# Prompt attention: even and odd key tiles of the value sums on the two column halves of TensorE

## The chip, the cores and the metric

The kernel runs on one core of one Trainium2 chip. The metric is the device time of one execution in microseconds (us). Each kernel is timed in several executions, and the median counts. One execution is also taken by the hardware profiler, and all rows of the trace come from that one.

## What is computed

The reference is one inference step of a decoder trunk of two layers, for a prompt of 1024 tokens and for a sample group of 8 sequences with 8 tokens each. The part that the change touches is the stick-breaking attention of the prompt in the first layer (8 heads of 64 channels, queries in blocks of 128, strictly causal). For each head and each block of queries it is, cut to what matters:

```python
z = jnp.einsum('nqhd,nkhd->nhqk', qblk, k) * scale + bias_f
mask = k_pos[None, :] < pblk[:, None]
log_1m = jnp.where(mask, jax.nn.log_sigmoid(-z), 0.0)
after = lax.cumsum(log_1m, axis=3, reverse=True) - log_1m
logw = jnp.where(mask, jax.nn.log_sigmoid(z) + after, -jnp.inf)
wgt = jnp.exp(logw)
return jnp.einsum('nhqk,nkhd->nqhd', wgt.astype(v.dtype), v)
```

The last line is the value sum: the weights of a block of 128 queries against all keys up to it, times the values of those keys. Around it stand the layer's projections, a convolution branch, the sample group's attention over a paged cache, output projections and feed-forward layers, all in float32.

## The kernel before

The program is one long stream of TensorE matmuls for the projections and feed-forward layers, in which weights are split into a high and a low part (tile `hl`, lines 184 to 197, ScalarE and GpSimd) and multiplied in three terms (`mm3`, line 235). Other work, which is called background here, is cut into pieces and put between those matmuls by hand: the generator `attention` (lines 937 to 1048) does a piece and yields, and the main stream asks for the next piece at fixed slots (`bg`, line 341). So each engine has a fixed order of instructions, written by the order in which Python issues them, and an engine that waits holds up all that is queued behind it.

Prompt attention runs in two halves: `attention(GA)` for the query blocks 0 to 3 (in the trace from about 230 to 338 us, beside the input projection of the second token group), `attention(GB)` for the blocks 4 to 7 (from there to about 564 us, beside the output projection and the feed-forward layer of the first token group). A unit is one head `h` and one query block `i`; it has i + 1 key tiles of 128 keys. The units of a half go head after head and within a head from the largest block down, so GA has 8 times (4, 3, 2, 1) key tiles, GB 8 times (8, 7, 6, 5).

Four stages work on a unit, one step of the loop in line 1029 apart:

- `s1(u)`: scores `z` by TensorE (line 982), and two sigmoids of them by ScalarE into `q` and `be` (line 987).
- `s2(u)`: VectorE runs the cumulative product backwards over the keys (`q`, lines 996 and 999, two scans) and multiplies it into `be` (line 1001).
- `s3(u)`: TensorE transposes `be` key tile by key tile (line 1011), ScalarE copies the result into `wt` (line 1012).
- `s4(u)`: TensorE adds up `vrow.T @ wt` over the key tiles into the PSUM tile `o` of 64 x 128 (line 1020), ScalarE copies `o` into the head's rows of `qall`, which is the upper half of `hb` (line 1021).

One step issues `s4(u - 3)`, `s3(u - 2)`, `s2(u - 1)` and `s1(u)`, with 12 matmuls of the main stream in between; for GB these 12 are cut in two groups of 6, one before `s1`, one behind. `o` has one buffer (`op_`, bufs=1), so the next unit's value sum may begin only when `o` has been read. `wt` also has one buffer, `q2` and `be` have two. The PE's instruction stream shows each float32 matmul of line 1020 as two records, so a unit of 8 key tiles has 16.

VectorE also serves the main stream: it moves accumulators `acc` out of PSUM (lines 291 and 295), forms low parts (lines 241 and 382), and prepares the next head's operands (lines 962 and 965). GpSimd forms the weights' low parts (line 186). The sample group's attention later in the program has, in `pv` (line 1210), matmuls to the row halves 0 to 63 and 64 to 127 of one PSUM tile, one after the other; they are not changed, but the prediction reads them.

Of the kernel before, what the change touches and what calls it, by code (L numbers as in the profile page):

```python
# [8 lines left out]
F = mybir.dt.float32  # L9
FR = mybir.dt.float32r  # L10
I32 = mybir.dt.int32
AF = mybir.ActivationFunctionType
OP = mybir.AluOpType
# [44 lines left out]
def trunk_kernel(ctx, tc, x_prompt, x_sample, cache_k, cache_v, state_conformer, state_shortconv, state_pool,  # L58
# [4 lines left out]
    pe, act, dve, pool, sp = nc.tensor, nc.scalar, nc.vector, nc.gpsimd, nc.sync  # L63
# [158 lines left out]
    def w_next(live=0):  # L222
        j = wj[0]
        wj[0] += 1
        w_split(j + 3 - live)
        w_load(need(j + 6 - live))
        return hls.pop(j)
# [408 lines left out]
    def accs():  # L636
        return accbox["p"].tile([128, len(accbox["g"].blocks), 512], F, name="acc")
# [8 lines left out]
    qall = hb[:, 4:8]  # L646
# [290 lines left out]
    def attention(g):  # L937
# [3 lines left out]
        with ExitStack() as es_:  # L941
            pa = es_.enter_context(tc.tile_pool(name=f"pa{g.c0}", bufs=1))
            zp = es_.enter_context(tc.tile_pool(name=f"zp{g.c0}", bufs=1, space=PSUM, side="right"))
            op_ = es_.enter_context(tc.tile_pool(name=f"op{g.c0}", bufs=1, space=PSUM, side="right"))
# [4 lines left out]
            kt_, qa, vrow, small = {}, {}, {}, []  # L949
# [64 lines left out]
            def s4(u):  # L1014
                h, i = units[u]
                hp, hh = divmod(h, 2)
                w = wt.pop(u)
                o = op_.tile([64, 128], F, name="o2")
                for j in range(i + 1):
                    pe.matmul(o, vrow[h][:, j], w[:, j], start=j == 0, stop=j == i)  # L1020
                act.activation(qall[hh * 64:hh * 64 + 64, hp, i * 128:i * 128 + 128], o, AF.Copy)

            load_v(0)
            operands(0)
# [4 lines left out]
            for u in range(len(units) + 3):  # L1029
                if u >= 3:  # L1030
                    s4(u - 3)
                if 2 <= u < len(units) + 2:
                    s3(u - 2)
                if 1 <= u < len(units) + 1:
                    s2(u - 1)
                if g is GB:
                    yield 1
                if u < len(units):
                    h, r = divmod(u, 4)
                    if r == 0 and h < 7:  # L1040
                        operands(h + 1)
                    if r == 2 and h < 7:
                        load_v(h + 1)
                    s1(u)
                for _ in range(2):
                    if small:
                        small.pop(0)()
                yield 1
# [672 lines left out]
    for n in range(2, KC):  # L1721
        h = w_next()
        a = accs()
# [4 lines left out]
    with tc.tile_pool(name="fab", bufs=1) as ep:  # L1728
        gen = forms_a(ep)
        for n in range(KC):  # L1730
            h = w_next()
            a = accs()
# [256 lines left out]
```

## Time and profile before

| what | value |
|---|---|
| median of 3 runs | 2576.84 us |
| lowest and highest run | 2574.14 and 2580.19 us |
| the profiled execution's own time | 2575.97 us |
| its span, first to last instruction | 2574.2 us |
| busy: TensorE matmul (PE), weight load (PEld) | 96% and 86% of the span |
| busy: VectorE (DVE), ScalarE (ACT), GpSimd (POOL) | 66%, 43%, 61% |
| mean granted TensorE clock | 0.994 |
| value sums, line 1020 | 576 matmul records, 238 to 564 us |

Shares of busy time are means over stages with different limits. Matmuls are pipelined, so the durations of neighbouring matmul records overlap, and the time that a run of them takes is read from the start of the first to the start of what comes next. In the rows of the timeline the first number is the start in us from the span's start, the second the time from the first start to the last end of the merged instructions; a bracket gives the idle time of the engine before it and who ended it. Rows of a window give its length, then the busy time of PE, PEld, DVE, ACT and POOL with the number of instructions, then granted clock, DMA share and GB/s.

### The profile page before, as it was taken

The page shows a single profiled execution, that of the slowest core. Times are in us where ns is not written, and L with a number is a line of the kernel's source. Part 1 is how long each engine was busy: PE and PEld are TensorE (multiplying, and loading weights), DVE is VectorE, ACT ScalarE, POOL GpSimd, SP SyncE. Part 2 cuts the span into 40 slices and gives each one's busy share as a digit, 9 for nine tenths or more (in the row PEclk, how much of TensorE's full clock was granted, in tenths as well). Part 3 has the DMA queues.
Part 4 walks back from the last instruction along what each step waited for, and adds up shares of the span by engine and source line. Part 5 has one row for each costly group of instructions (what it writes and reads, how often), then busy time and mean ns, then how long its engine had stood idle before and what let it go on. Part 6 is the DMA issues. An engine that isn't in the chain of part 4 may idle for free.

```text
span 2574.2 us, 41142 instructions
## 1 busy us (share of the span) xinstructions
PE 2477.7 (96%) x15727; PEld 2213.7 (86%) x15727; DVE 1693.0 (66%) x2359; ACT 1105.3 (43%) x1875; POOL 1564.2 (61%) x1205
## 2 busy tenths in 40 slices
PE   8999999999999999999999999999999998999998
PEld 6788877887777668989999889989888887999997
DVE  3696777968867734467666633348776778666655
ACT  5536766754444334334333522234434434443333
POOL 6754243544434346678777722266888885887775
PEclk9999999999999999999999999999999999999999
DMA  7342231224555434222323411152233332333322
GB/s 220 113 113 74 64 109 46 70 83 142 157 162 160 139 107 152 74 74 83 99 83 98 130 42 46 38 161 65 84 91 96 95 96 82 107 95 103 99 83 78
DMA packets 355484, 258.30 MB, mean 100 GB/s; under 512 B 22913, under 2 KB 303617, under 8 KB 355272
## 3 DMA queue, kind: packets, MB, share of 16 engines
q1 hardware_dynamic: 355256, 255.66, 33.8%
q8 instruction: 125, 2.05, 0.3%
q14 instruction: 71, 0.58, 0.1%
q10 hardware_dynamic: 32, 0.01, 0.0%
HBM read 237.41 MB, written 18.69 MB: 99 GB/s over the span
## 4 chain that ended last, share of the span: by engine, by line
PE 44%; DVE 8%; POOL 2%; issue 1%; ACT 1%; POOLq 0%; DVEq 0%; ACTq 0%
PE acc L235 23%; PE acc L521 20%; POOL hl L197 1%; DVE sum L200 1%; DVE hid L241 1%; DVE hb L295 1%; DVE sum L201 1%; DVE b L1669 0%; DVE tmp L525 0%; DVE sum L202 0%; DVE x L1669 0%; DVE sum_c L214 0%; DVE fb L1673 0%; DVE xs L1673 0%; POOL tmp L500 0%
## 5 line engine op out<-in xcount | busy, mean ns | idle before, releaser
L186 POOL TENSOR_TENSOR hl<-stage,hl 128x512 fp32r<-128x512 f32 x464 | 634.7, 1391 | 475.1 <-ACT hl L184 357.0
L235 PE MATMUL acc<-x,hl 128*128 128x512 f32 (+1 forms) x3648 | 780.6, 350 | 12.2 <-DVE hb L295 2.6
L235 PEld LDWEIGHTS acc<-x,hl 128*128 128x128 f32 x3648 | 581.4, 189 | 77.2 <-issue 10.9
L235 PE MATMUL acc<-hid,hl 128*128 128x288 f32 (+1 forms) x3096 | 552.3, 334 | 16.8 <-DVE hb L295 6.9
L235 PEld LDWEIGHTS acc<-hid,hl 128*128 128x128 f32 x3096 | 470.4, 190 | 69.9 <-DVE hb L295 11.0
L295 DVE TENSOR_TENSOR hb<-acc,hb 128x512 f32<-128x512 f32 (+1 forms) x360 | 256.4, 718 | 184.8 <-PE acc L235 183.4
L521 PE MATMUL acc<-x,hl 128*128 128x288 f32 (+1 forms) x2676 | 362.4, 290 | 6.0 <-ACT x L1792 2.0
L521 PEld LDWEIGHTS acc<-x,hl 128*128 128x128 f32 x2676 | 349.0, 188 | 8.4 <-POOL hl L197 2.7
L197 POOL TENSOR_TENSOR hl<-sum,hl 128x512 fp32r<-128x512 f32 x180 | 237.1, 1344 | 168.6 <-ACT hl L196 168.5
L184 ACT ACTIVATE hl<-stage 128x1024 fp32r<-128x1024 f32 x232 | 243.5, 1055 | 218.5 <-PE acc L235 129.6
L525 DVE TENSOR_TENSOR tmp<-acc,tmp 128x288 f32<-128x288 f32 (+1 forms) x420 | 173.5, 441 | 228.0 <-ACT tmp L537 135.3
L197 POOL TENSOR_TENSOR hl<-stage,hl 128x512 fp32r<-128x512 f32 x180 | 267.0, 1505 | 13.3 <-ACT hl L196 13.3
L521 PE MATMUL acc<-b,hl 128*128 128x256 f32 (+1 forms) x1548 | 216.6, 291 | 14.1 <-DVE tmp L525 11.2
L521 PEld LDWEIGHTS acc<-b,hl 128*128 128x128 f32 x1548 | 202.3, 189 | 19.6 <-ACT hl L196 12.7
L235 PE MATMUL acc<-x1t,hl 128*128 128x288 f32 x1152 | 216.4, 296 | 1.5 <-POOL hl L186 1.5
L235 PEld LDWEIGHTS acc<-x1t,hl 128*128 128x128 f32 x1152 | 196.0, 188 | 19.4 <-POOL hl L186 1.7
L196 ACT ACTIVATE hl<-sum 128x512 fp32r<-128x512 f32 x180 | 103.1, 623 | 237.9 <-DVE sum L202 217.6
L291 DVE TENSOR_TENSOR tmp<-acc,rr 128x512 f32<-128x512 f32 (+1 forms) x108 | 75.0, 709 | 113.2 <-PE acc L235 100.0
L500 POOL TENSOR_TENSOR tmp<-tmp 128x576 f32<-128x576 f32 (+1 forms) x85 | 127.8, 1504 | 11.7 <-ACT tmp L477 8.3
L196 ACT ACTIVATE hl<-stage 128x512 fp32r<-128x512 f32 x180 | 105.6, 618 | 67.5 <-PE acc L235 62.3
L241 DVE TENSOR_TENSOR hid<-tmp,hid 128x512 fp32r<-128x512 f32 (+1 forms) x88 | 99.1, 1127 | 44.0 <-ACT hid L240 41.2
L235 PE MATMUL acc<-x1a,hl 128*128 128x512 f32 x480 | 121.7, 407 | 2.5 <-POOL hl L186 1.3
(289 smaller groups left out, 3242.9 us busy)
## 6 DMA issues: line engine op xcount, KB each, us to landing
stage<-in_w_ffn_in_dram SPq DMA_DIRECT2D x176, 512.0 KB
stage<-in_w_ffn_out_dram SPq DMA_DIRECT2D x88, 512.0 KB
stage<-in_w_in_even_dram SPq DMA_DIRECT2D x40, 512.0 KB
kst<-in_cache_k_dram SPq DMA_DIRECT2D x64, 256.0 KB
vst<-in_cache_v_dram SPq DMA_DIRECT2D x64, 256.0 KB
stage<-in_w_out_even_dram SPq DMA_DIRECT2D x16, 512.0 KB
stage<-in_w_in_odd_dram SPq DMA_DIRECT2D x16, 512.0 KB
stage<-in_w_out_odd_dram SPq DMA_DIRECT2D x16, 512.0 KB
```

The lines of the kernel that those rows point to most:

```text
L184: act.activation(hl[:, 0], st, AF.Copy)
L186: pool.tensor_tensor(hl[:, 1, c], st[:, c], f32(hl[:, 0, c]), op=OP.subtract)
L196: act.activation(hl[:, 0, c], x, AF.Copy)
L197: pool.tensor_tensor(hl[:, 1, c], x, f32(hl[:, 0, c]), op=OP.subtract)
L200: todo = [lambda: dve.tensor_tensor(sb, su[:, lo], su[:, hi], op=OP.add), lambda: dve.tensor_tensor(sa[:, hi], sg[:, lo], su[:, lo], op=OP ...
L235: pe.matmul(acc[:, b, :c1 - c0], w, xs[:, xi, c0 - o:c1 - o], start=first and s == 0, stop=last and s == 2)
L241: (on or dve).tensor_tensor(dst[:, 1], src, f32(dst[:, 0]), op=OP.subtract)
L291: dve.tensor_tensor(d, a, r, op=OP.mult)
L295: dve.tensor_tensor(d, a, d, op=OP.add)
L500: (dve if both and f == NF - 1 else pool).tensor_tensor(t[:, :n], t[:, :n], u[:, :n], op=OP.mult)
L521: pe.matmul(acc[:, :w2], h[:, wi, i, k], xk[:, xi], start=k == 0 and s == 0, stop=k == 3 and s == 2)
L525: dve.tensor_tensor(out, acc[:, :w2], x, op=OP.add)
```

## The change

Only `s4` is changed. The PSUM tile is 128 x 128 instead of 64 x 128. Key tile j goes to its lower 64 partitions where j is even and to its upper 64 where j is odd, which puts the matmul on the one or the other column half of the array; each half accumulates its own sum (so the first matmul of each half starts it, and the last of each half stops it). Where a unit has one key tile, ScalarE copies as before. Elsewhere ScalarE copies the odd half into a new SBUF tile `ot` (two buffers), and VectorE adds the even half from PSUM to it and writes the result to `qall`.

```diff
-                o = op_.tile([64, 128], F, name="o2")
+                o = op_.tile([128, 128], F, name="o2")
                 for j in range(i + 1):
-                    pe.matmul(o, vrow[h][:, j], w[:, j], start=j == 0, stop=j == i)
-                act.activation(qall[hh * 64:hh * 64 + 64, hp, i * 128:i * 128 + 128], o, AF.Copy)
+                    pe.matmul(o[j % 2 * 64:j % 2 * 64 + 64], vrow[h][:, j], w[:, j], start=j < 2, stop=j >= i - 1)
+                r = slice(hh * 64, hh * 64 + 64)
+                a = qall[r, hp, i * 128:i * 128 + 128]
+                if i == 0:
+                    act.activation(a, o[0:64], AF.Copy)
+                    return
+                t = pa.tile([128, 128], F, name="ot", bufs=2)
+                act.activation(t[r], o[64:128], AF.Copy)
+                dve.tensor_tensor(a, o[0:64], t[r], op=OP.add)
```

On TensorE, ScalarE, GpSimd and SyncE the instructions stand in the same order as before, with the same counts; ScalarE's copy of line 1021 is now that of line 1027 (or 1024 for one key tile). VectorE has 56 instructions more, one for each unit but the 8 with one key tile.

On VectorE in the first half of attention (GA), in a step with a unit of four key tiles, the difference is this (`qz` is the next head's operand, the number in `o_2256` is that of the buffer; the order names a scan SCALAR_TENSOR_TENSOR where the trace says TENSOR_TENSOR_SCAN):

```order
 L1001 TENSOR_TENSOR be<-be,q_2196 128x383
 L965 TENSOR_TENSOR qz_2107<-hb,qa 64x512
+L1028 TENSOR_TENSOR hb<-o_2256,ot 64x128
 L996 SCALAR_TENSOR_TENSOR q_2231<-q_2231,ident 128x128
 L999 SCALAR_TENSOR_TENSOR q_2231<-q_2231,ones 128x128
 L1001 TENSOR_TENSOR be<-be,q_2231 128x255
```

The sum of the older unit, three steps behind, stands ahead of the scans of the unit that is one step behind.

On VectorE in the second half (GB), the order before over three steps of a head reads as follows.

```order
L965 TENSOR_TENSOR qz_3521<-hb,qa 64x512
L996 SCALAR_TENSOR_TENSOR q_4822<-q_4822,ident 128x128
L999 SCALAR_TENSOR_TENSOR q_4822<-q_4822,ones 128x640
L1001 TENSOR_TENSOR be<-be,q_4822 128x767
L291 TENSOR_TENSOR tmp<-acc,rr 128x512
L996 SCALAR_TENSOR_TENSOR q_4871<-q_4871,ident 128x128
L999 SCALAR_TENSOR_TENSOR q_4871<-q_4871,ones 128x512
L1001 TENSOR_TENSOR be<-be,q_4871 128x639
L996 SCALAR_TENSOR_TENSOR q_4931<-q_4931,ident 128x128
```

And the same place with the change:

```order
L965 TENSOR_TENSOR qz_3569<-hb,qa 64x512
L1028 TENSOR_TENSOR hb<-o_4923,ot 64x128
L996 SCALAR_TENSOR_TENSOR q_4910<-q_4910,ident 128x128
L999 SCALAR_TENSOR_TENSOR q_4910<-q_4910,ones 128x640
L1001 TENSOR_TENSOR be<-be,q_4910 128x767
L291 TENSOR_TENSOR tmp<-acc,rr 128x512
L1028 TENSOR_TENSOR hb<-o_4978,ot 64x128
L996 SCALAR_TENSOR_TENSOR q_4961<-q_4961,ident 128x128
L999 SCALAR_TENSOR_TENSOR q_4961<-q_4961,ones 128x512
L1001 TENSOR_TENSOR be<-be,q_4961 128x639
L1028 TENSOR_TENSOR hb<-o_5036,ot 64x128
L996 SCALAR_TENSOR_TENSOR q_5023<-q_5023,ident 128x128
```

Each step's first scan now has the add ahead of it.

ScalarE's order in those steps, with the change, shows what stands ahead of the copy that the add needs:

```order
L1027 ACTIVATE ot<-o_4978 64x128
L1012 ACTIVATE wt<-m 128x512
L1012 ACTIVATE wt<-m 128x256
L184 ACTIVATE hl<-stage 128x1024
L987 ACTIVATE q_5023<-z_5018,bh 128x1024
L987 ACTIVATE be<-z_5018,bh 128x1024
L959 ACTIVATE kt<-kall 64x1024
L960 ACTIVATE qa<-hb 64x512
L1027 ACTIVATE ot<-o_5036 64x128
```

Nothing moved here; before, the copies of line 1021 stood in these places.

## The prediction

> **What bounds the kernel now.** I read the profile's page first.
>
> ```profile
> span 2574.2 us, 41142 instructions
> PE 2477.7 (96%) x15727; PEld 2213.7 (86%) x15727; DVE 1693.0 (66%) x2359; ACT 1105.3 (43%) x1875; POOL 1564.2 (61%) x1205
> ```
>
> TensorE is busy nearly all the time, but this is a mean. What the value sums are worth is read from the stretch in which they stand. So next came the value sums' own line: its matmuls, and who waited for them.
>
> ```profile
> L1020 PE MATMUL o<-wt,vrow x576: 272/273/325, 238.2 to 563.7; 128*64 128x128 f32 x192
> ACT hb L1021: 35.2, 34
> ```
>
> ScalarE's copy is the only one that often waits for them (35.2 us in 34 waits); it is on no critical path so far, because nothing near needs its result. Then the table by stretch, one row for each head of the second half, from the first value sum of a head to that of the next (length, then busy PE, PEld, DVE, ACT, POOL):
>
> ```profile
> 359.00:384.54 25.54, 23.97 (x144) 19.72 (x143) 24.50 (x20) 17.45 (x29) 15.49 (x12) 1.00 0.31 83
> 384.54:409.87 25.33, 25.33 (x149) 20.85 (x149) 20.26 (x19) 17.72 (x29) 13.30 (x12) 1.00 0.20 53
> 409.87:449.75 39.88, 36.59 (x196) 28.54 (x195) 28.88 (x33) 25.03 (x40) 12.69 (x13) 1.00 0.14 40
> 449.75:474.39 24.64, 24.20 (x143) 19.71 (x142) 23.62 (x19) 18.74 (x30) 15.92 (x14) 1.00 0.31 86
> 474.39:498.33 23.94, 23.94 (x144) 19.74 (x143) 20.88 (x19) 16.88 (x28) 9.59 (x12) 1.00 0.20 55
> 498.33:522.26 23.93, 23.93 (x144) 19.73 (x143) 20.78 (x19) 17.11 (x28) 9.56 (x11) 1.00 0.20 56
> 522.26:546.19 23.93, 23.93 (x143) 19.73 (x142) 19.94 (x23) 14.50 (x24) 8.24 (x10) 1.00 0.15 45
> 546.19:563.80 17.61, 17.61 (x111) 14.54 (x110) 8.93 (x9) 7.41 (x15) 5.91 (x6) 1.00 0.21 60
> ```
>
> TensorE fills five of these heads without a gap, so its time is the heads' length there. But VectorE is close behind: 20.8 of 23.9 us in the two middle ones, 24.50 of 25.54 and 23.62 of 24.64 in two others, where TensorE already has gaps. The clock is 1.00 and the DMA share at most 0.31, so neither limits. Nothing later runs to a fixed time; what TensorE gains here stays.
>
> **What is removed: TensorE time.** The timeline gives the runs of line 1020, first for one head of the first half, then for one of the second:
>
> ```profile
> 302.19 1.09 PE L1020 MATMUL o<-wt,vrow 128*64 128x128 f32 x8
> 305.51 0.87 PE L1020 MATMUL o<-wt,vrow 128*64 128x128 f32 x6
> 308.75 0.65 PE L1020 MATMUL o<-wt,vrow 128*64 128x128 f32 x4
> 312.08 0.43 PE L1020 MATMUL o<-wt,vrow 128*64 128x128 f32 x2
> ...
> 498.33 1.96 PE L1020 MATMUL o<-wt,vrow 128*64 128x128 f32 x16
> 504.54 1.74 PE L1020 MATMUL o<-wt,vrow 128*64 128x128 f32 x14
> 510.75 1.52 PE L1020 MATMUL o<-wt,vrow 128*64 128x128 f32 x12
> 516.50 1.31 PE L1020 MATMUL o<-wt,vrow 128*64 128x128 f32 x10
> ```
>
> Each record costs 0.109 us ((1.96 - 1.09) / 8). Do two column halves run at the same time? The same program has a case: the sample group's matmuls alternate between the two halves.
>
> ```profile
> 679.37 1.94 PE L1210 MATMUL o<-vst,wts 128*64 128x512 f32 x8
> ```
>
> Eight records of 512 columns, at 4 x 0.109 = 0.436 us each, would take 7 x 0.436 + 0.59 = 3.64 us one behind another (0.59 being one record alone); as four pairs 3 x 0.436 + 0.59 = 1.90. The row says 1.94: they run in pairs. So a run's time becomes that of its longer half. For 8, 7, 6, 5 key tiles these are 4, 4, 3, 3 tiles, that is 8, 8, 6, 6 records: 1.96, 1.74, 1.52, 1.31 become 1.09, 1.09, 0.87, 0.87, which saves 0.87, 0.65, 0.65, 0.44, in all 2.61 us a head. For 4, 3, 2, 1 key tiles it saves 0.44, 0.22, 0.22 and 0, in all 0.88. Eight heads each: 20.9 + 7.0 = 27.9 us. The surplus of 0.04 us over four slots would, on 320 slots, take back 3.2 at most; I take none, since a like start is in the rows of line 1020 already.
>
> **What is added: 56 adds on VectorE.** No row has this form (64 x 128, one input from PSUM). The nearest:
>
> ```profile
> L1149 DVE TENSOR_TENSOR zs<-z,zs x24: 410/540/552, 589.5 to 891.5; 64x384 f32<-64x384 f32 x16, 64x264 f32<-64x264 f32 x8
> L965 DVE TENSOR_TENSOR qz<-hb,qa x16: 677/689/1769, 229.8 to 523.8; 64x512 fp32r<-64x512 f32 x16
> L291 DVE TENSOR_TENSOR tmp<-acc,rr x10: 677/686/693, 444.7 to 562.8; 128x512 f32<-128x512 f32 x10
> L996 DVE TENSOR_TENSOR_SCAN q<-q,ident x64: 406/420/1539, 232.1 to 554.3; 128x128 f32<-128x128 f32 x64
> ```
>
> Line 1149 is the same operation on 264 and 384 columns: 0.410 and about 0.540 us, a slope of 0.0011 us a column, so 0.26 to 0.27 for 128. The far bound is line 996, also 128 columns wide, which takes up to 1.54 us when it meets GpSimd. I take 0.27, since line 291, with one input from PSUM like the add, never left 0.677 to 0.693, while line 965, with both inputs in SBUF, went to 1.77. That is 56 x 0.27 = 15.1 us of VectorE, 1.08 in a head of the second half. With 1.54 it would be 86 us.
>
> [...]
>
> ScalarE's copy keeps its size and place: no cost. GpSimd, SyncE and the DMA queues keep their order. TensorE's next value sum now also waits for the add, since `o` has one buffer; that is a whole step later (5 to 6 us), so it costs nothing.
>
> **The new wait.** Before, VectorE's scans of the unit one step behind started whenever VectorE was free. Now the add stands ahead of them, and it waits for ScalarE's copy, which waits for this step's value sum and for all that ScalarE has queued. Behind it wait the scans, the product `be`, and the accumulators' moves; TensorE's transposes of the next step wait for `be`. I worked through the head from 498.33, from VectorE's, ScalarE's and GpSimd's timelines and TensorE's transposes:
>
> ```profile
> 505.25 1.13 DVE L996 TENSOR_TENSOR_SCAN q<-q,ident 128x128 f32<-128x128 f32 x1
> 508.64 0.82 DVE L1001 TENSOR_TENSOR be<-be,q 128x639 f32<-128x639 f32 x1
> 510.60 1.54 DVE L996 TENSOR_TENSOR_SCAN q<-q,ident 128x128 f32<-128x128 f32 x1 [1.14 <-ACT q L987]
> 514.39 1.23 DVE L1001 TENSOR_TENSOR be<-be,q 128x1023 f32<-128x1023 f32 x1
> 517.67 0.69 DVE L241 TENSOR_TENSOR hid<-tmp,hid 128x512 fp32r<-128x512 f32 x1 [0.73 <-ACT hid L240]
> 521.19 2.00 DVE L1001 TENSOR_TENSOR be<-be,q 128x895 f32<-128x895 f32 x1
> ```
> ```profile
> 505.37 0.63 ACT L474 ACTIVATE tmp<-tmp 128x512 f32<-128x512 f32 x1 [0.65 <-DVE tmp L291]
> 506.31 0.27 ACT L1021 ACTIVATE hb<-o 64x128 f32<-64x128 f32 x1 [0.32 <-PE o L1020]
> 513.08 0.25 ACT L1021 ACTIVATE hb<-o 64x128 f32<-64x128 f32 x1
> ```
> ```profile
> 508.86 3.00 POOL L186 TENSOR_TENSOR hl<-stage,hl 128x512 fp32r<-128x512 f32 x2 [1.41 <-ACT hl L184]
> ```
> ```profile
> 512.20 0.77 PE L1011 MATMUL m<-ident,be 128*128 128x128 f32 x5
> 517.74 1.09 PE L1011 MATMUL m<-ident,be 128*128 128x128 f32 x8
> ...
> 524.15 0.98 PE L1011 MATMUL m<-ident,be 128*128 128x128 f32 x7
> ```
>
> Step from 504.54: the copy cannot start before line 474 has ended (506.0), so copy and add end at 506.58; the scan before started at 505.25, so it is 1.33 late. Its `be` ended at 509.46, the transposes came at 512.20: 2.74 of slack, of which TensorE's own gains in this step and the next take 1.30. What is left, 1.44, covers it.
>
> Step from 510.75: ScalarE is busy until the copy at 513.08 to 513.33, and this is not TensorE's doing. The add ends at 513.60; the scan started at 510.60, before TensorE had even begun this value sum. It is 3.0 late. It then no longer meets GpSimd's line 186 (over at 511.86), which may give back 1.13 (1.54 against 0.41): 1.87. Slack: 517.74 - 515.62 = 2.12, less 1.09 of gains: 1.03. TensorE stalls 0.84.
>
> Step from 516.50: 1.03 of lateness is left, a gap of 0.73 on VectorE takes most of it, the add brings 0.27: 0.57. Slack: 524.15 - 523.19 = 0.96, less gains of 1.31: -0.35. TensorE stalls 0.92. The fourth step has slack enough.
>
> So of 2.61 us the head keeps 2.61 - 0.84 - 0.92 = 0.85. In VectorE's terms its length becomes 23.08 = 20.78 + 1.08 + 1.22, where 1.22 is the waiting that the add brings.
>
> **The sum.** I carry that to the other heads: new length is the larger of (length - 2.61) and (VectorE's busy time + 1.08 + 1.22). In the order of the rows above the gains are -1.26, 2.61, 2.61, -1.28, 0.76, 0.85, 1.69, 2.61: 8.6 us. In the first half the gain lies between 0 and 0.88 a head. Its low end is seen here, where the transposes already follow `be` by 0.06 us and every gain turns into waiting:
>
> ```profile
> 242.55 0.42 DVE L1001 TENSOR_TENSOR be<-be,q 128x255 f32<-128x255 f32 x1
> ...
> 243.03 0.44 PE L1011 MATMUL m<-ident,be 128*128 128x128 f32 x2 [0.58 <-DVE be L1001]
> ```
>
> I take 0.3, nearer to this row, since the add delays VectorE in these steps too: 2.4 us. Together 11.0 us. The profiled execution (2575.97, its span 2574.2 and 1.8 around it) would come to 2565.0; the median, 0.87 higher, to 2565.8.
>
> **Rivals.** A measurement of this kernel can tell about 0.2%, 5.2 us, from no change.
>
> (1) *TensorE keeps nearly all.* The waits for the copy vanish into gaps, as VectorE's lateness also delays what GpSimd and ScalarE do. With 0 in place of 1.22 the heads give 0, 2.61, 2.61, -0.06, 1.98, 2.07, 2.61, 2.61, in all 14.4, and the first half 7.0: 21.4 us, 2555.4. For it: the one 1.13 shows that GpSimd's meetings can move either way. Against it: the copy at 513.08 is late through ScalarE alone.
>
> (2) *Slower: VectorE, waiting for ScalarE's copy, becomes the bound.* If no lateness is absorbed, a head of VectorE grows by 0.27 + 1.33 + 3.0 + 0.27 = 4.87, so waiting is 3.8 in place of 1.22. The heads give -3.84, 0.19, 2.61, -3.86, -1.82, -1.73, -0.89, 2.61: -6.7, the first half 0, so 2583.5. It decides from a waiting of about 2.7 us a head. For it: the two heads with VectorE at 24.50 and 23.62 us have no room at all; against it: 1.14 and 0.73 us gaps in the head above. [...]
>
> (3) *The halves do not run together here*, because a 128-column pass hides two weight loads less well than line 1210's 512. Then the 27.9 us are gone; the lateness costs 2.5 us in the two full heads and about 0.5 in five others: 2581.8. Against it: line 1210.
>
> (4) *Nearly nothing*: waits between my 1.22 and rival 2's, within 5 us of before.
>
> **Numbers.** Forecast (5 to 17 us less) 0.48; (1) 0.15; (2) 0.16; (3) 0.04; (4) 0.17. Faster 0.63, same 0.18 (with a part of (3)), slower 0.19. The range leaves out little of (1) and the far part of (2): 2554 to 2582.
>
> **What would show it.** Line 1020's runs of 16 records at about 1.1 us prove the pairing; 1.9 would prove rival 3. The add of 64 x 128 should show 0.27 us and wait for line 1027 in most steps; TensorE's transposes should wait for `be` in several steps of each head, by 1 to 2 us. If these waits are absent, rival 1 holds; if VectorE is busy or waiting for ScalarE without a gap through most heads, rival 2.

## The result and the profile after

The changed kernel takes 2590.4 us (median of 4 runs, 2588.63 to 2592.99) against 2576.49 before (4 runs). The ratio is 1.0052, with a 95% interval of 1.0037 to 1.0068: slower by half a per cent, where 11 us less had been forecast. The profiled execution has a span of 2587.4 us, 13.2 more than before. Three executions of the kernels tried below, whose granted clock fell to between 0.65 and 0.85, are left out of every median and ratio.

The page after, first lines:

```profile
span 2587.4 us, 41236 instructions
PE 2460.0 (95%) x15727; PEld 2195.4 (85%) x15727; DVE 1701.4 (66%) x2415; ACT 1107.9 (43%) x1875; POOL 1565.6 (61%) x1205
```

TensorE's busy time fell by 17.7 us while the span grew by 13.2: TensorE has less to do and waits more. (Line 1020 alone fell by more, from 76.6 to 48.9 us.) VectorE's busy time rose by 8.4 us only, less than the adds themselves take, so its other operations became 7.5 us shorter together. Half of that is line 500, long after attention (6.9 to 3.2 us); of attention's own lines the product (1001) lost 3.5 us and the long scan (999) gained 2.3.

The value sums' line, their runs of 16 and 14 records in the timeline, and the add's line:

```profile
L1020 PE MATMUL o<-wt,vrow x576: 272/273/325, 237.6 to 579.8; 128*64 128x128 f32 x192
...
536.29 1.09 PE L1020 MATMUL o<-wt,vrow 128*64 128x128 f32 x16
546.86 1.09 PE L1020 MATMUL o<-wt,vrow 128*64 128x128 f32 x14
```
```profile
L1028 DVE TENSOR_TENSOR hb<-o,ot x56: 271/283/286, 238.9 to 580.4; 64x128 f32<-64x128 f32 x56
its engine sat idle before it (us, times) until:
  ACT ot L1027: 42.0, 28
```

The pairing is there in full: 1.96 and 1.74 us became 1.09 and 1.09. The add costs 0.283 us. But VectorE stood still for 42.0 us in front of it, waiting for ScalarE's copy. And the waits behind it show who pays: TensorE's transposes wait 37.1 us for the product `be` (us in all, times, longest), against 3.0 us in 3 waits before. Here the row before, then the row after:

```profile
PE m L1011 <- DVE be L1001: 3.0, 3, 1.6
```
```profile
PE m L1011 <- DVE be L1001: 37.1, 33, 3.7
```

The first value sum starts 0.6 us earlier than before, the last 16.1 us later (579.8 against 563.7).

By heads of the second half, from one head's first value sum to the next one's, as before:

```profile
364.79:390.04 25.25, 21.57 (x144) 17.12 (x143) 21.14 (x21) 16.68 (x27) 14.31 (x13) 1.00 0.32 85
390.04:418.36 28.32, 24.49 (x149) 19.55 (x149) 21.65 (x23) 18.52 (x30) 10.19 (x11) 0.94 0.21 58
418.36:459.25 40.89, 35.36 (x195) 27.05 (x194) 29.62 (x39) 25.72 (x40) 11.58 (x12) 0.96 0.11 32
459.25:488.14 28.89, 23.90 (x144) 19.30 (x143) 24.88 (x23) 19.80 (x31) 15.49 (x13) 0.88 0.26 73
488.14:511.51 23.37, 21.45 (x143) 17.14 (x142) 20.07 (x23) 17.13 (x28) 11.41 (x12) 1.00 0.21 57
511.51:536.29 24.78, 21.39 (x143) 17.12 (x143) 20.45 (x23) 17.23 (x28) 10.36 (x11) 1.00 0.19 54
536.29:562.85 26.56, 22.90 (x143) 18.44 (x143) 23.83 (x27) 14.60 (x24) 8.56 (x10) 0.94 0.12 41
```

These seven heads took 25.54, 25.33, 39.88, 24.64, 23.94, 23.93 and 23.93 us before. Two are shorter now (by 0.29 and 0.57), five longer (by 2.99, 1.01, 4.25, 0.85, 2.63). In each longer one, TensorE and VectorE both have gaps (24.49 and 21.65 busy of 28.32): neither is the bound, they wait for each other in turn. And in four of them the granted clock is below 1.00, which it was in none before.

How the turn looks in the first half, in TensorE's, ScalarE's, VectorE's and again TensorE's timeline of the changed kernel:

```profile
300.49 0.44 PE L1020 MATMUL o<-wt,vrow 128*64 128x128 f32 x4
```
```profile
300.68 0.62 ACT L960 ACTIVATE qa<-hb 64x512 fp32r<-64x512 f32 x1
301.32 0.28 ACT L1027 ACTIVATE ot<-o 64x128 f32<-64x128 f32 x1
```
```profile
301.63 0.28 DVE L1028 TENSOR_TENSOR hb<-o,ot 64x128 f32<-64x128 f32 x1 [2.71 <-ACT ot L1027]
...
308.32 1.09 DVE L996 TENSOR_TENSOR_SCAN q<-q,ident 128x128 f32<-128x128 f32 x1
309.44 1.31 DVE L999 TENSOR_TENSOR_SCAN q<-q,ones 128x128 f32<-128x128 f32 x1
310.86 0.42 DVE L1001 TENSOR_TENSOR be<-be,q 128x255 f32<-128x255 f32 x1
```
```profile
311.34 0.44 PE L1011 MATMUL m<-ident,be 128*128 128x128 f32 x2 [0.94 <-DVE be L1001]
```

VectorE idles 2.71 us. For the first 2.0 of them the value sum is not done (it ends at 300.93): TensorE is itself late, having stood still for 1.35 us at 298.06 for an earlier `be`. Only the next 0.4 us are ScalarE's, which does the next head's operands (line 960) ahead of the copy, and the last 0.3 are the copy. From here VectorE works without a gap: two steps on, the scans run beside GpSimd (1.09 and 1.31 us; with GpSimd idle the same forms took 0.41 at 298.12 and 0.48 at 296.99) and TensorE waits 0.94 us for `be`. And the worst place, in the second half:

```profile
534.33 0.28 DVE L1028 TENSOR_TENSOR hb<-o,ot 64x128 f32<-64x128 f32 x1
534.65 1.56 DVE L996 TENSOR_TENSOR_SCAN q<-q,ident 128x128 f32<-128x128 f32 x1
536.25 2.65 DVE L999 TENSOR_TENSOR_SCAN q<-q,ones 128x768 f32<-128x768 f32 x1
538.93 1.97 DVE L1001 TENSOR_TENSOR be<-be,q 128x895 f32<-128x895 f32 x1
```
```profile
534.64 2.64 POOL L186 TENSOR_TENSOR hl<-stage,hl 128x512 fp32r<-128x512 f32 x2 [4.03 <-DVE hb L1028]
...
537.28 2.68 POOL L500 TENSOR_TENSOR tmp<-tmp 128x512 f32<-128x512 f32 x1
```
```profile
541.05 1.73 PE L1011 MATMUL m<-ident,be 128*128 128x128 f32 x7 [3.66 <-DVE be L1001]
```

Here the add does not wait itself; VectorE is still late from the add before, which waited 2.10 us for its copy (at 527.46). The late scan meets GpSimd for its whole length, and TensorE stands still for 3.66 us. Then the transposes themselves are slow: 1.73 us for 7 where before the row read 0.98. The window that follows shows why (length, then the five busy times, then the granted clock):

```profile
541.00:544.40 3.40, 3.35 (x12) 3.00 (x13) 3.30 (x6) 1.07 (x2) 0.00 (x0) 0.51 0.02 5
544.40:549.00 4.60, 4.60 (x35) 3.74 (x34) 3.58 (x7) 2.12 (x4) 0.10 (x1) 1.00 0.00 0
```

The clock is 0.50 for 3.4 us, from 540.9, just ahead of the stall's end, to 544.3. In these heads the same came with the stalls of 2.79, 2.60 and 3.51 us that end at 393.97, 445.64 and 463.85: 0.50 from 394.2 to 397.5, from 445.4 to 448.7 and, for 6.8 us, from 462.4 to 469.2. Around those of 2.43 and 2.29 us that end at 368.31 and 514.90 it stayed at 1.00. What sets the slow clock off is not shown here.

### The profile page after: what moved, and what is told of

Its sections match the earlier page's. It is cut to its first block, busy times and chain, and to the rows that moved or that the text cites. A ratio compares the mean times of both kernels' runs of the same rounds, so it can differ in the third digit from the quotient of the medians.

```text
span 2587.4 us, 41236 instructions
## 1 busy us (share of the span) xinstructions
PE 2460.0 (95%) x15727; PEld 2195.4 (85%) x15727; DVE 1701.4 (66%) x2415; ACT 1107.9 (43%) x1875; POOL 1565.6 (61%) x1205
## 4 chain that ended last, share of the span: by engine, by line
PE 43%; DVE 9%; POOL 2%; issue 1%; ACT 1%; POOLq 0%; DVEq 0%; ACTq 0%
PE acc L235 23%; PE acc L521 19%; POOL hl L197 1%; DVE sum L200 1%; DVE hid L241 1%; DVE hb L295 1%; DVE sum L201 1%; DVE sum L202 0%; DVE tmp L525 0%; DVE sum_c L214 0%; DVE b L1676 0%; POOL tmp L500 0%; DVE fb L1680 0%; PE blk L1899 0%; DVE x L1676 0%
```

## The experiments

Three theories stood. A: the add stands ahead of the scans and makes them wait for ScalarE's copy. B: VectorE has no room for 56 more operations, wherever they stand. C: the value sums' PSUM tile has one buffer, and the next value sum waits for the add. In a kernel's edit, `sums_` is a list of held-back adds: the add of line 1028 becomes

```diff
-                dve.tensor_tensor(a, o[0:64], t[r], op=OP.add)
+                sums_.append(lambda: dve.tensor_tensor(a, o[0:64], t[r], op=OP.add))
```

and `while sums_: sums_.pop(0)()` issues it at the place named.

**The add at the end of the step's attention work** (the two lines behind `s2(u - 1)` in the loop).

> The add of the changed kernel is issued at the end of the step's VectorE work for attention, behind the scans and the product be, in place of ahead of them; everything else is as in the changed kernel. Theory A (the add, standing ahead of the scans, makes them wait for ScalarE's copy, and the transposes wait for be): VectorE's wait for line 1027 falls from 42 us to under 8, TensorE's wait for be from 38 us to under 15, and most of the 27.9 us of TensorE time is kept: 2552 to 2563 us. Theory B (VectorE is simply too full for 56 more operations, 15.9 us, wherever they stand): 2585 to 2592, as with the change. Theory C (the PSUM tile of the value sums has one buffer, and the next value sum waits for the add): above 2590, with a wait of TensorE for the add in the trace.

2571.67 us against 2574.82; ratio 0.9986 (0.9976 to 0.9996). All three theories missed the time. The waits of TensorE between 229 and 590 us:

```profile
PE o L1021 <- DVE hb L1029: 11.3, 9, 2.2
PE o L1021 <- ACT qa L964: 6.4, 4, 1.7
PE m L1012 <- DVE be L1002: 2.6, 2, 2.4
...
PE o L1021 <- ACT be L988: 1.2, 2, 0.9
PE o L1021 <- ACT hl L184: 1.2, 1, 1.2
```

A is right on `be` (2.6 us in place of 37.1), and C is right on what replaces it: the value sums (line 1021 here) wait for the add that frees their PSUM tile. The profile puts 11.3 us down to the add and 8.8 to ScalarE, but all 16 value sums of these rows start 0.10 to 0.15 us behind the end of an add, so this wait is 20.1 us. B is out: the same 56 adds stand here in a kernel that is 0.66%, some 17 us, faster than the changed one.

**The add between the scans and `be`** (the two lines in `s2`, ahead of line 1001).

> The add is issued between the scans and the product be. Theory A: by then the copy has been done nearly everywhere, so be is late only by the add's own 0.28 us: 2553 to 2565 us, 0 to 4 us above the kernel with the add behind be. Theory B: 2585 to 2592. Theory C: between the changed kernel and the kernel with the add behind be, since the PSUM tile is freed between the two.

2557.61 us; ratio 0.9934 (0.9920 to 0.9948). In A's range of time; but A had put it 0 to 4 us above the kernel with the add behind `be`, and C between that kernel and the changed one, and it is 0.52% below the former. Where the change waited for 42.0 us, this kernel's add waits 9.4, and TensorE waits 7.8 us for `be` and 7.6 for PSUM (5.8 and 1.5 in the rows below and 0.3 more; these value sums too start right behind an add):

```profile
PE m L1014 <- DVE be L1004: 7.8, 11, 2.4
PE o L1023 <- DVE hb L1031: 5.8, 5, 1.6
...
PE o L1023 <- ACT hid L240: 1.5, 1, 1.5
...
DVE hb L1031 <- ACT ot L1030: 9.4, 19, 1.7
```

**The add between the short and the long scan** (the two lines ahead of line 997).

> The add stands between the step's first, short scan (line 996) and the long one (line 999), so PSUM is freed about 1 to 2.5 us earlier than with the add between the scans and be, but the copy has had only 0.4 us more to come than in the change. Theory A with C (the add waits for ScalarE's copy if it stands too early, TensorE's next value sum waits for the add if it stands too late): worse than the kernel with the add right before be (2557.6), since most of the copy's lateness is over 0.4 us: 2570 to 2586. If the place before be is already too late for PSUM: below 2557.

Ratio 1.0014 (1.0006 to 1.0023), median 2580.11 us against 2575.44. Within A's range. VectorE waits 25.1 us for the copy again, TensorE 27.3 us for `be`, only 2.3 for PSUM:

```profile
DVE hb L1031 <- ACT ot L1030: 25.1, 24, 1.8
...
PE m L1014 <- DVE be L1004: 27.3, 28, 2.4
PE o L1023 <- DVE hb L1031: 2.3, 2, 1.1
```

The four places in one line: ahead of the scans 1.0052, between them 1.0014, before `be` 0.9934, behind `be` 0.9986. Two waits work against each other, and each is there in the trace: in the same order TensorE waits 37.1, 27.3, 7.8 and 2.6 us for `be`, and 0, 2.3, 7.6 and 20.1 us for the PSUM tile. The sums, 37.1, 29.6, 15.4 and 22.7 us, order the four kernels as their times do. A second buffer for `o`, which would take away the second wait, was not tried.

**The halves alone.** The odd half's sum is left out; only the even half is copied, by ScalarE.

```diff
-                if i == 0:
-                    act.activation(a, o[0:64], AF.Copy)
-                    return
...
-                act.activation(t[r], o[64:128], AF.Copy)
-                dve.tensor_tensor(a, o[0:64], t[r], op=OP.add)
+                act.activation(a, o[0:64], AF.Copy)
```

> The value sums go to the two column halves as in the change, but only the even half is copied, by ScalarE as before the change; the odd half's sum is left out and there is no add. This gives TensorE's gain alone. Theory A: VectorE's order is that of before, so nearly all of the 27.9 us comes: 2549 to 2557 us. Rival (VectorE's scans bound attention already, add or no add): 2562 to 2572 us, with TensorE waiting 10 us or more for be.

2557.66 us; ratio 0.9931 (0.9916 to 0.9946): 0.69%, or 17.8 us of the 27.9, between the two theories' ranges. TensorE waits for `be` 10.8 us, where it was 3.0 before the change:

```profile
PE m L1011 <- DVE be L1001: 10.8, 13, 2.4
```

So VectorE's scans take back some 8 us of TensorE's gain even without an add. And the kernel with the add before `be`, which computes everything, is as fast as this one (0.9934): there the adds and their waits cost nothing that can be measured.

**The wait without the halves.** The sum stays on one half; VectorE takes the maximum of it and of its copy.

```diff
-                act.activation(qall[hh * 64:hh * 64 + 64, hp, i * 128:i * 128 + 128], o, AF.Copy)
+                if i == 0:
+                    act.activation(a, o, AF.Copy)
+                    return
+                t = pa.tile([128, 128], F, name="ot", bufs=2)
+                act.activation(t[r], o, AF.Copy)
+                dve.tensor_tensor(a, o, t[r], op=OP.max)
```

> The value sums stay on one column half as before the change, but ScalarE copies the sum to ot and VectorE writes the maximum of the sum and its copy (the same value) at the add's place, ahead of the scans. So the wait and the operation are there, and TensorE's gain isn't. Theory A: the scans are as late as with the change, but the transposes also come later by what TensorE no longer saves, so part of the 38 us of waiting for be goes: 2584 to 2600 us. Theory B: 15.9 us of VectorE time, partly in gaps: 2578 to 2583.

2586.95 us; ratio 1.0042 (1.0027 to 1.0058). As A said. VectorE waits 44.9 us for the copy, as long as with the change, but TensorE waits only 16.1 us for `be`:

```profile
DVE hb L1028 <- ACT ot L1027: 44.9, 32, 2.6
...
PE m L1011 <- DVE be L1001: 16.1, 18, 2.2
```

**The same maximum between the scans and `be`.**

> No halves; ScalarE's copy and VectorE's maximum as in the kernel with the maximum alone (2587), but the maximum stands between the scans and be. Theory A: at this place the operation costs next to nothing: 2573 to 2579, as before the change. Theory B: 2583 to 2588.

2576.67 us against 2575.21; ratio 1.0006 (0.9997 to 1.0015): not to be told from no change, as A said. So moving the operation is worth 1.0042 - 1.0006 = 0.36% without the halves, and 1.0052 - 0.9934 = 1.18% with them. The halves bring TensorE to each transpose sooner, and a `be` that is late by about the same amount then stalls it longer (37.1 us against 16.1). A part of the difference may be the clock, whose mean in the second half is 1.00 with the maximum and 0.96 with the change; this was not separated.

**The operation without the wait, first try.** The halves alone, and at the change's place 56 adds of constants.

```diff
+                if i:
+                    t = pa.tile([128, 128], F, name="ot", bufs=2)
+                    dve.tensor_tensor(t[r], ident[r], ones[r], op=OP.add)
```

> As the kernel with the halves alone (the odd half's sum is left out), and at the change's place, ahead of the scans, VectorE adds two constant tiles of 64 x 128 that wait for nothing. So VectorE's 56 operations and their place are there without the wait. Theory A (the wait, not the operation or its place in itself): 2557 to 2564 us, at most 56 x 0.28 = 15.7 us less gaps above the 2557.7 of the halves alone. Theory B (VectorE's time): 2573 or more, the whole 15.7 us or above.

Ratio 0.9973 (0.9964 to 0.9982), 2568.76 us: between the theories, and not a fair test, because these adds have both inputs in SBUF and went up to 1.4 us (17 of the 56 took 1.25 us or more):

```profile
L1026 DVE TENSOR_TENSOR ot<-ident,ones x56: 273/290/1412, 240.1 to 559.5; 64x128 f32<-64x128 f32 x56
```

**Second try, with the change's form.** The added operand is the unit's scores in PSUM.

```diff
+                z = zt.pop(u)
+                if u > 1 and units[u - 2][1]:
+                    t = pa.tile([128, 128], F, name="ot", bufs=2)
+                    dve.tensor_tensor(t[0:64], z[0:64, 0, 0:128], ones[0:64], op=OP.add)
```

> As the kernel with the halves alone (odd half left out), and ahead of the scans 56 adds of the form of the change's (64 x 128, one input from PSUM, one from SBUF), which read the scores of the unit that the scans belong to, and so wait for nothing that the scans don't wait for. The constant adds of the earlier run had two SBUF inputs and 20 of 56 took over 1.2 us; these should all take 0.27 to 0.29. Theory A: the wait for the copy made the loss, and VectorE's 15.9 us at this place cost a few us: 2558 to 2566. Theory B, that the place itself costs, since every scan is 0.28 us later: 2568 or more. TensorE's next scores may wait for the add now and then, which the trace would show.

2562.69 us; ratio 0.9948 (0.9934 to 0.9961), in A's range, and 0.0017, some 4 us, above the halves alone; the two intervals overlap. The adds took 0.27 to 0.28 us each (53 of them; this edit has none for the last units of each half):

```profile
L999 DVE TENSOR_TENSOR ot<-z,ones x53: 271/276/284, 238.8 to 542.5; 64x128 f32<-64x128 f32 x53
```

Of the changed kernel's distance to the halves alone (1.0052 - 0.9931 = 1.21%), some 0.17% is the operation at its place, and rather less, since TensorE also waited 4.0 us here for the scores' PSUM that these adds read, which the change doesn't have. The rest is the wait and what follows from it. The pair also bears on the prediction's comparison of lines 965 and 291: two SBUF inputs took 1.412 us at most, one input from PSUM 0.284 at most, at the same place of the step.

**VectorE copies the odd half itself.** In the change, `act.activation(t[r], o[64:128], AF.Copy)` becomes `dve.tensor_copy(t[r], o[64:128])`.

> The change with its add ahead of the scans, but VectorE itself copies the odd half to SBUF in place of ScalarE, so VectorE has 112 operations more and waits only for TensorE's value sum, not for what ScalarE has queued. If ScalarE's queue made most of the 42 us of waiting: 2570 to 2582 us. If TensorE's value sum did (the add meets the unit whose sum this step has just issued): no better than the change, 2588 to 2605.

Ratio 1.0023 (1.0014 to 1.0033), 2581.22 us against 2575.44, in the first of the two ranges. VectorE now waits 14.4 us for the value sum in place of 42.0 for the copy:

```profile
DVE ot L1027 <- PE o L1020: 14.4, 14, 1.6
```

So, by this run, about a third of the 42.0 us came from the value sum itself and the rest by way of ScalarE. The changed kernel's own trace says it more exactly: with each of its 28 waits cut at the end of the value sum and at the start of the copy, 17.5 us pass before the value sum has ended, 16.0 while ScalarE is busy with other work, and 8.4 with the copy itself. The halves of attention differ: in the first, 15.7 of 21.6 us are the value sum; in the second, 1.7 of 20.3, and 13.1 are ScalarE's other work. The kernel is better than the change although VectorE has 112 operations more than before.

**Only the second half of attention**, with the add before `be`; the first half (`if g is GA`) keeps one column half and ScalarE's copy.

> The halves and the add (between scans and be) in the second half of attention alone; the first half is as before the change. Theory A: the second half has 20.9 of the 27.9 us of TensorE time; the first half's 7.0 are partly lost where its transposes already followed be closely. 2557 to 2563 us; if the first half's steps give nothing or cost something, at or below the 2557.6 of both halves.

2562.46 us; ratio 0.9950 (0.9937 to 0.9963). In range. The first half is then worth about 0.16% more, 4 of its 7.0 us; the intervals of the two kernels overlap.

**Units of two key tiles left as they were** (`i <= 1`), add before `be`.

> The kernel with the add between the scans and be, but units of two key tiles keep one column half and ScalarE's copy (they save 0.22 us of TensorE time each, 1.8 in all, and their adds go). In the first half of attention, steps behind the largest unit waited up to 1.6 us for the PSUM tile; if the adds of these small units matter for that, 2553 to 2557; if not, 2557 to 2560, since their 1.8 us are given up.

2558.42 us; ratio 0.9933 (0.9919 to 0.9946), against 0.9934: no difference, in the second of the two ranges. The version that beats both kernels stays the one with the add between the scans and `be`, faster than before by 0.66%.

## Why the prediction was wrong

*TensorE's gain, 27.9 us:* right as a count (1.96 to 1.09 us and so on; line 1020's busy time fell by 27.7), too high as what can be had. The halves alone give 17.8 us, as `be` then comes too late. Rival 1's ceiling of 21.4 us was near that.

*The add, 0.27 us, 15.1 in all:* right (0.283), and by itself nearly free.

*The copy and the PSUM tile at no cost:* right at the place that the change gives the add. It is not free in general: behind `be` it costs 20.1 us of waiting.

*The new wait:* the mechanism was named, with the right partners; the size failed. The step that failed is the waiting of 1.22 us a head, worked out for the head from 498.33 and then carried to all the others. Three things in it were wrong.

First, the working of that head never asked what a late scan would newly meet. It forecast two stalls of TensorE, 0.84 and 0.92 us. At the same transposes the changed kernel waits 1.09 us (531.80) and 3.66 us (541.05). The first was sized well: as forecast, the late scan at 527.78 missed GpSimd (0.42 us). The second was not. Before, the scans of that step stood here (the product behind them, from 521.19, is shown in the prediction):

```profile
518.88 0.41 DVE L996 TENSOR_TENSOR_SCAN q<-q,ident 128x128 f32<-128x128 f32 x1
519.33 1.82 DVE L999 TENSOR_TENSOR_SCAN q<-q,ones 128x768 f32<-128x768 f32 x1
```

Scans and product took 4.31 us then, and 6.25 from 534.65, where they met lines 186 and 500 of GpSimd one after the other: 1.94 us that no term of the forecast had. They also began 1.64 us ahead of the next value sum in place of 3.38, so 1.74 late, where the forecast's 0.57 of lateness and 0.44 of TensorE's gain make 1.01. The two together are the 2.7 us by which this stall exceeds 0.92. The same step a head earlier cost 2.29 us (at 514.90). That the change should have kept this head 0.85 us shorter and the next one 1.69, while they are 0.85 and 2.63 us longer, is this step.

Second, the waiting was carried by a rule that has no term for two engines that wait for each other: a head's new length was the larger of TensorE's total and VectorE's total. Lateness did die in VectorE's old gaps: these were waits for ScalarE's sigmoids, 23.2 us before and 3.4 after, so that the adds' 42.0 us (28 of 56 adds) are 22.2 more for the 16 heads of the two halves, or 1.4 a head. But where VectorE had room in total, the rule let a head lose nothing, and there the forecast was far off: the second and third rows were put at the full gain of 2.61 us each and came out 2.99 and 1.01 longer. In the seven rows together 6.0 us were to be gained and 10.9 were lost.

Third, the first half was put at a gain of 0.3 us a head from one quoted place. It lost: the first value sum of the second half begins 5.8 us later than before (364.79 against 359.00), where 2.4 less had been forecast. With steps of some 3 us a wait of 2.71 is nearly a step, and most of the waiting there was for a value sum that TensorE, waiting for `be`, began late. From there to the last value sum 10.3 us more were lost (16.1 - 5.8), where 8.6 less had been forecast.

The signs that the prediction named for itself came: runs at 1.09 us, adds at 0.28, waits for line 1027 (in half of the steps, not in most), 33 waits for `be` of 1.1 us in the mean. They could not tell it from rival 2.

Rival 2, given 0.16, had the sign, and was right that lateness would not be absorbed; but VectorE did not become the bound, as the heads' rows show. Its 2583.5 fell short for the first and third reasons, and for a term that no rival had: the clock of 0.50 at four stalls (2.60 to 3.66 us). From the heads' rows that is at most 1.7 + 1.6 + 3.5 + 1.6 = 8.4 us (length times the missing share of the clock). How much of it is part of the loss was not separated by a run. In the second half of attention the mean clock is 0.98 with the halves alone, 0.96 with the change, and 1.00 with the maximum ahead of the scans, which is 0.42% slower than before without any of it. The three rows in that order:

```profile
345.00:550.00 205.00, 192.76 (x1214) 152.66 (x1213) 179.84 (x162) 145.34 (x230) 97.46 (x86) 0.98 0.23 64
```
```profile
345.00:580.00 235.00, 205.81 (x1247) 163.44 (x1247) 187.24 (x203) 153.56 (x241) 95.38 (x90) 0.96 0.24 67
```
```profile
345.00:577.00 232.00, 217.49 (x1239) 176.25 (x1240) 186.45 (x204) 152.20 (x243) 96.82 (x90) 1.00 0.24 69
```

So 205 x 0.02 = 4 us of missing clock with the halves alone, and 235 x 0.04 = 9 us with the change.

*Rival 3* (the halves don't run together) is out by the runs of line 1020: 16 records in 1.09 us, with weight loads (PEld) for 0.85 us of it (1.96 and 1.72 before).

The span grew by 13.2 us though the last value sum came 16.1 later. The 3 us came back far from attention: up to 2130 us of the kernel before, TensorE's same instructions are 16.4 us later with the change, and from 2135 us 13.7. Between them VectorE's line 500, which runs beside GpSimd's line 186 in both, took 5.37 us before and 1.64 after, and line 241 behind it 1.47 and 3.47. Whether the kernel before has the long form in every execution is not shown; in the profiles of all other kernels here line 500 took 1.6 to 1.7 us there. So some 0.1% of each ratio may come from this place.

## What to carry to other kernels

When a new operation is put into an in-order queue, its place counts more than its length: put it behind the work that a busy engine waits for, as soon as its own input is surely there, and no later than the buffer that it frees is wanted. Here the same 56 adds cost 1.2% ahead of the scans and nothing between the scans and `be`. A gain on the busiest engine also shortens the slack of everything that it waits for, so a late producer costs more after the gain than before it (moving the operation was worth 0.36% without the halves, 1.18% with them).

## What the runs showed of the hardware

Two column halves with 128-column float32 passes ran in pairs here as fully as those with 512 columns: 16 records in 1.09 us, the time of 8 on one half before; 8 records of 512 columns (line 1210) in 1.94, where four pairs were reckoned at 1.90. A stall of TensorE had a second price in four places: with 3.66 us of waiting came a granted clock of 0.51 for 3.4 us, and seven transposes took 1.73 us in place of 0.98. Not each stall had it: with one of 2.60 us the clock fell to 0.50, with one of 2.43 us it stayed at 1.00. A VectorE add of 64 x 128 took up to 1.41 us with two inputs in SBUF (the first try above) and never over 0.29 with one of them in PSUM (0.286 at most in the change, 0.284 in the second try).
